# Two-layer decoder trunk on one core: gate columns' product, trips, residual and first loads rescheduled; spread of maxima 128 rows deep; gate statistics turned by two products

## The chip, the cores and the metric

The kernel runs on 1 core of one Trainium2 chip. The metric is the time of one execution in microseconds; the median of 3 runs of the kernel before is 1042.13 us (1041.74 to 1042.76).

## The reference

A sequence of 256 tokens, 2048 features wide, passes two layers. All is float32.

```python
hn = rmsnorm(h, norm)
# layer 0: u = hn @ e_w_in (six column groups: q, f, i, za, xb, zb of 1024)
ya = head_rmsnorm(hgrn2(q, f, i), a_norm) * silu(za)   # gated linear recurrence, 8 heads
yb = rg_lru(causal_conv(xb)) * silu(zb)                # elementwise recurrence
h = h + concat(ya, yb) @ e_w_out
# layer 1: u = hn @ o_w_in (qk 2048, v 2048, og 2048, z 2048, ig 8, fg 8)
li = ig + c_b_i;  lf = log_sigmoid(fg + c_b_f)
yc = mlstm(silu(conv(qk)), v, li, lf)                  # matrix memory, running-max stabiliser
yc = head_rmsnorm(yc, c_norm) * sigmoid(og) * silu(z)
h = h + yc @ o_w_out
# after each layer's mixer
pl = rmsnorm(p[i] @ ple_w[i], ple_norm[i])
h = h + sigmoid(h @ ple_gate_w[i]) * pl
# at the end: rmsnorm(h, final_norm)
```

The 16 gate columns `ig`, `fg` of the second layer give per head a log input gate and a log forget gate. From them come, per head and token, the running maximum `Mx`, the exponents `av` and the floor `enm` of the denominator.

## The kernel before, in words

**The large products.** Every weight matrix is cut into quarters of 128 partitions by 2048 values, each loaded by `load_weights` as two transfers of 512 KB into `raw` (5 buffers) on the queue of SyncE (SP). Each float32 weight is split into `whi` (a cast on ScalarE, L132) and `wlo` (raw minus whi, on VectorE, L133); the activations are split the same way. `quarter_tok` then issues three matmuls for each pair of 128 features and half of the tokens: hi x hi (L193), hi x lo (L194), lo x hi (L195), each 128 rows deep and 512 columns wide. A block of 512 output columns (`project_tok`) is four quarters, 96 matmuls. `whi` and `wlo` have 4 buffers each, so two quarters.

**Who sets the order.** The program is written for a scheduler that puts each engine's instructions into one fixed stream. Side work is written as generators in named lanes; `pump()`, called once in each quarter, advances every lane by one step, and places what the step emits behind the last instruction of TensorE, ScalarE, VectorE and the last trip (`last["pe"]`, `last["act"]`, `last["dve"]`, `last["hop"]`). `tc.issue_after(x)` puts an instruction behind `x` in the order.

**Trips.** Between token-major and feature-major layout a block goes out to DRAM and back (`across`, L452 the store, L455 four loads), issued by GpSimd (POOL). A trip's user continues after `lag` steps of its lane. `gated_mix` (L804) multiplies the trip of `zb` with the recurrence's result; `feature_major` (L483) scales and splits the other half of the first mixer's output.

**The start.** `embed` multiplies the first 256-wide input with two weight blocks `pw` of 2048 columns. The first block is loaded in pieces (four of 256 columns, two of 512), some on ScalarE's queue (`s`), the rest on SP's (`sy`); the first half of the second block in two pieces of 512, the last in one of 1024. Then come the blocks of `ew`.

**The end of layer 0.** `hq` is the residual, four blocks of 512 KB loaded by POOL at L865. `out_proj` adds the product `eo` to it (L374, on VectorE). Behind the first `eo` block the space of pool `m0` is closed and used again by pool `e0`: the rows of gains (`row`, L322, loaded by POOL, used at L329), the gate columns `gr` (L882, loaded by SP) and `wg` (L885, VectorE: `gr` times the norm's gains). `wg` is used first by `gate_sums` (L896), in the block after `eo`.

**The gate statistics.** `gate_stats` computes `li`, `lf`, `Mx`, `av`, `enm` as 8 rows of 256 and turns `av` and `enm` to tokens x heads by four small float32 products with the identity (L1001, 8 rows deep; a float32 product is two passes in the trace). `split_rows` puts `Mx` into rows 0 to 7 and its rounding rest into rows 32 to 39 of the tile `s`, rows 8 to 31 are zero. For each pair of heads `spread` (L233) copies one head's row to all 128 partitions by a product of 40 rows with `identr`, twice for each of the four calls of `mix`; L1052 are the products with the values that stand ahead of the next pair's spread.

Of the kernel before, what the change touches and what calls it, by code (L numbers as in the profile page):

```python
# [11 lines left out]
F32 = mybir.dt.float32  # L12
# [4 lines left out]
ALU = mybir.AluOpType  # L17
# [26 lines left out]
def trunk(ctx: ExitStack, tc: tile.TileContext, a, out):  # L44
# [72 lines left out]
        return pc(name, 0, PRM[name][1])  # L117


    def load_weights(src, pieces=(1, 1), queues=8 * (sy,)):  # L120
        parts = []
        for hf in range(2):
            raw = wp.tile([P, 1024], F32, name="raw", tag="raw", bufs=5)
            hi = wp.tile([P, 1024], F32R, name="whi", tag="whi")
            lo = wp.tile([P, 1024], F32R, name="wlo", tag="wlo")
            n = 1024 // pieces[hf]
            for c in range(0, 1024, n):
                r, h, l = (x[:, c:c + n] for x in (raw, hi, lo))
                queues[hf * 4 + c // n].dma_start(out=r, in_=src[:, hf * 1024 + c:hf * 1024 + c + n])
                with ExitStack() as order:  # L130
                    order.enter_context(tc.high_priority(offset=400))
                    last["act"] = s.copy(h, r).ins  # L132
                    last["dve"] = v.tensor_tensor(out=l, in0=r, in1=h.bitcast(F32), op=ALU.subtract).ins  # L133
            parts.append((hi, lo))
        return parts
# [86 lines left out]

    def split_rows(x):

        both = tp.tile([P, T], F32R, name="s8", tag="dg", bufs=1)[0:40]
        v.memset(both.bitcast(F32), 0.0)
        v.tensor_copy(both[0:8], x)
        v.tensor_tensor(out=both[32:40], in0=x, in1=both[0:8].bitcast(F32), op=ALU.subtract)
        return both

    def spread(o, both, h):

        te.matmul(o, identr[:, h:h + 1].to_broadcast([40, P]), both, start=True, stop=True)  # L233

    def free_copy(rt, name):
        ps = to_free(rt)
# [35 lines left out]
    def embed(w, pact, tile_of, first=None):  # L272

        pls = []
        for b in range(2):
            head = first and b == 0
            parts = load_weights(w[b], *((((4, 2), (s, s) + 6 * (sy,)) if head else ((2, 1),)) if first else ()))
            if first and b:
                first()
            for c, (hi, lo) in enumerate(parts):  # L280
                terms = [(hf, k, x, y) for hf in range(2) for k in range(2) for x, y in ((0, 0), (0, 1), (1, 0))]
                if head:
                    terms.sort(key=(lambda t: (t[3], t[3] and t[0], t[1])) if c == 0 else
                               (lambda t: (t[1], t[3] if t[1] == 0 else t[0], t[3])))
                pool, name = (px, "mx") if head and c == 0 else (pm, "mm")
                ps = [pool.tile([P, 512], F32, name=name, tag=name) for _ in range(2)]
                halves = []
                for n, (hf, k, x, y) in enumerate(terms):
                    mine = [m for m, t in enumerate(terms) if t[0] == hf]
                    with ExitStack() as behind:  # L290
                        if first and "pe" in last:
                            behind.enter_context(tc.issue_after(last["pe"]))
                        last["pe"] = te.matmul(ps[hf], tokens(pact[x], k, hf), (hi, lo)[y][:, k * 512:(k + 1) * 512],  # L293
                                               start=(n == mine[0]), stop=(n == mine[-1])).ins
                    if n < mine[-1]:
                        continue
                    pl = tile_of()
                    with ExitStack() as order:
                        if first:
                            order.enter_context(tc.high_priority(offset=600))  # L300
                        if hf and (b or not first):
                            v.tensor_copy(pl, ps[hf])
                        else:
                            s.copy(pl, ps[hf])
                    halves.append(pl)
                pls.append(halves)
        return pls
# [87 lines left out]
    def small(n, name, rows=P):  # L395
# [7 lines left out]
    m0 = m0_scope.enter_context(tc.tile_pool(name="m0", bufs=2))  # L403
    pls = embed(a["pw"], load_p(0), lambda: p0.tile([P, 512], F32, name="pl", tag="pl"),
                lambda: sy.dma_start(out=prm, in_=a["prm"]))
    identr = cp.tile([40, 8], F32R, name="identr")
    acth = []
    xt = [hp.tile([P, 1024], F32, name="xt", tag="h") for _ in range(4)]
    xss = cp.tile([P, 2, 2], F32, name="xss")
# [50 lines left out]
    def landed(u, name, lag):  # L460

        w = room("w")
        w5 = w.rearrange("p (j c h t) -> p h c j t", j=4, c=4, h=2)
        for hf in range(2):
            v.transpose(w5[:, hf], u[hf].rearrange("p (c j q) -> p c j q", c=4, j=4))  # L465
        r = room("r")
        yield from across(w, r, name, lag)
        return r
# [72 lines left out]
    if True:  # L541
# [254 lines left out]

        def gated_mix(j, u):

            r = yield from landed((u[:, 0], u[:, 1]), f"dzb{j}", 6 - j)
            while ("h", j) not in res:  # L800
                yield
            for b in range(2):
                x = tp.tile([P, 512], F32, name="xr", tag="hn", bufs=3)
                v.tensor_tensor(out=in_order(x, 0, 2), in0=as_read(r, 2 * b, 2),  # L804
                                in1=in_order(res["h", j], 2 * b, 2), op=ALU.mult)
                y[4 + 2 * j + b] = split_act(x, "y")
# [12 lines left out]
        def combine():  # L819
            for g in [g for g in held if ("o", g) in res]:  # L820
                u = held.pop(g)
                for hf in range(2):
                    v.tensor_tensor(out=u[:, hf], in0=u[:, hf], in1=res["o", g][:, hf], op=ALU.mult)
                start(f"fm{g}", feature_major(u, "an", 4 * g, y, 5))

        for g in range(2):
            start(f"f{g}", f_use(g, scaled_tok(2 * g, None if g else load_x)))
# [31 lines left out]
            step(f"fm{2 + g}")  # L859
        drain("rg", "pl")  # L860
    hq = []
    for i in range(4):
        t = hp.tile([P, 2, 512], F32, name="hq", tag="h")
        with tc.issue_after(last["hop"]):
            gp.dma_start(out=t, in_=a["x"].rearrange("(h p) f -> p h f", h=2)[:, :, i * 512:(i + 1) * 512])  # L865
        hq.append(t)

    def mixed():
        for c, ps in enumerate(chunks(a["eo"], 4, y, ready(y, "fm"))):
            if c == 0:  # L870
                m0_scope.close()
                pe0.append(l0.enter_context(tc.tile_pool(name="e0", bufs=1)))
                start("pg", ple_gain(pls, row(pe0[0], "row", 2, 0)))
            yield ps
# [7 lines left out]
    sy.dma_start(out=gr, in_=a["ogf"])  # L882
    wt = e0.tile([P, KT, 32], F32, name="wg")
    gp.memset(wt, 0.0)
    v.tensor_tensor(out=wt[:, :, 0:16], in0=gr, in1=pall("on").unsqueeze(2).to_broadcast([P, KT, 16]), op=ALU.mult)  # L885
    gps = px.tile([P, 512], F32, name="mx", tag="mx")

    held5 = []
# [32 lines left out]
    with tc.tile_pool(name="m1", bufs=2) as m1:  # L921
# [45 lines left out]
            return m1.tile([8, T], F32, name=name, bufs=1)  # L967

        li, xf, ab, Bc, Mx = (t8(n) for n in ("li", "xf", "ab", "Bc", "Mx"))
        lf, av, enm = xf, li, Bc  # L970
        aT = m1.tile([P, 32], F32, name="aT", bufs=1)
        pM = []

        def gate_stats():
            yield
            ps = px.tile([P, 512], F32, name="mx", tag="mx")
            te.matmul(ps[0:40, 0:T], gsum, gm, start=True, stop=True)
            cbi = prm[0:8, PRM["cbi"][0]:PRM["cbi"][0] + 1]
            cbf = prm[0:8, PRM["cbf"][0]:PRM["cbf"][0] + 1]
            for x, c, b in ((li, 0, cbi), (xf, 32, cbf)):  # L980
                v.tensor_tensor(out=x, in0=ps[c:c + 8, 0:T], in1=norm["rs"][c:c + 8], op=ALU.mult)
                v.tensor_scalar(x, x, b, None, op0=ALU.add)
            s.activation(ab, xf, AF.Abs)
            s.activation(ab, ab, AF.Exp, scale=-1.0)
            v.tensor_scalar(ab, ab, 1.0, None, op0=ALU.add)
            s.activation(ab, ab, AF.Ln)
            v.scalar_tensor_tensor(lf, xf, 0.0, ab, op0=ALU.min, op1=ALU.subtract)
            v.tensor_tensor_scan(Bc, ones[0:8, :], lf, 0.0, op0=ALU.mult, op1=ALU.add)
            v.tensor_tensor(out=av, in0=li, in1=Bc, op=ALU.subtract)
            v.tensor_tensor_scan(Mx, ones[0:8, :], av, 0.0, op0=ALU.mult, op1=ALU.max)  # L990
            v.tensor_tensor(out=enm, in0=Bc, in1=Mx, op=ALU.add)
            s.activation(enm, enm, AF.Exp, scale=-1.0)
            pM.append(split_rows(Mx))
            yield
            yield
            yield
            px_ = px.tile([P, 512], F32, name="mx", tag="mx")
            for c, x in ((0, av), (16, enm)):
                for hf in range(2):
                    o = c + hf * 8  # L1000
                    te.matmul(px_[:, o:o + 8], x[:, hf * P:(hf + 1) * P], ident[0:8, 0:8], start=True, stop=True)  # L1001
            v.tensor_copy(aT, px_[:, 0:32])

        start("mix", gate_stats())

# [333 lines left out]
```

## Time and profile before

| | |
|---|---|
| median of 3 runs | 1042.13 us (1041.74 to 1042.76) |
| the profiled execution's own time | 1042.44 us |
| its span in the trace | 1040.7 us |
| TensorE busy | 1030.2 us, 99% |
| weight loads busy | 854.7 us, 82% |
| VectorE busy | 730.4 us, 70% |
| ScalarE busy | 601.7 us, 58% |
| GpSimd busy | 90.1 us, 9% |
| HBM read, written | 216.02 MB, 17.83 MB |

Times in a trace count from the span's start. A matmul's start is recorded, its end is modelled, and matmuls overlap, so that the distance from one start to the next tells the rate, not the duration. "PEld" is TensorE loading weights. A bracket behind a row is the engine's idle time ahead of it and what ended that.

### The profile page before, as it was taken

The numbers are of one execution on the slowest core, as the hardware profiler recorded it, in microseconds if no ns is written. First come the engines' busy times: TensorE is split into PE (matmuls) and PEld (weight loads), VectorE is DVE, ScalarE is ACT, GpSimd is POOL, SyncE is SP. The second block draws the span as 40 slices with busy tenths as digits, with TensorE's granted clock in tenths as the row PEclk, the third lists the DMA queues.
The fourth block names the chain that finished last, engine by engine and source line by source line (L and its number), as shares of the span: only waits on it lengthen the run. The fifth ranks groups of instructions, "written<-read, shape, count | busy, mean of one in ns | idle before, by whom it ended". The sixth has DMA issues, their size and how long they took to land.

```text
span 1040.7 us, 14521 instructions
## 1 busy us (share of the span) xinstructions
PE 1030.2 (99%) x5278; PEld 854.7 (82%) x5278; DVE 730.4 (70%) x1101; ACT 601.7 (58%) x887; POOL 90.1 (9%) x171
## 2 busy tenths in 40 slices
PE   9999999999999999999999999999999999999996
PEld 7888888888888888888788788888888888888886
DVE  7858878969685775777569976555457777666675
ACT  7675555587974444565557765644445557344553
POOL 0111101001121211111021000000001110111000
PEclk9999999999999999999999999999999999999999
DMA  9977646567779877687587654455557778788552
GB/s 343 342 246 228 222 160 210 179 202 232 234 247 313 288 248 242 212 276 239 179 268 253 201 173 153 162 183 186 198 195 230 247 257 284 240 251 247 195 182 82
DMA packets 67752, 234.80 MB, mean 226 GB/s; under 512 B 8800, under 2 KB 10080, under 8 KB 67680
## 3 DMA queue, kind: packets, MB, share of 16 engines
q1 hardware_dynamic: 55728, 196.64, 56.9%
q0 software_dynamic: 11520, 36.71, 11.7%
q8 instruction: 41, 0.67, 0.3%
q10 hardware_dynamic: 432, 0.52, 0.1%
q14 instruction: 31, 0.25, 0.1%
HBM read 216.02 MB, written 17.83 MB: 225 GB/s over the span
## 4 chain that ended last, share of the span: by engine, by line
PE 91%; issue 4%; DMA 2%; ACT 1%; POOL 1%; DVE 0%; ACTq 0%; DVEq 0%; POOLq 0%; SPq 0%
PE mm L193 25%; PE mm L194 25%; PE mm L195 25%; PE mx L195 3%; PE mx L193 3%; PE mx L194 3%; PE mm L293 2%; DMA gr<-in_ogf_dram 1%; PE nu L1052 1%; DMA r<-dzb 1%; PE mm L1180 1%; PE mm L1179 1%; PE mm L1178 1%; DMA dzb<-w 1%; POOL r L455 1%
## 5 line engine op out<-in xcount | busy, mean ns | idle before, releaser
L133 DVE TENSOR_TENSOR wlo<-raw,whi 128x1024 fp32r<-128x1024 f32 (+2 forms) x365 | 437.7, 1207 | 228.7 <-ACT whi L132 215.9
L132 ACT CAST whi<-raw 128x1024 fp32r<-128x1024 f32 (+2 forms) x365 | 378.9, 1041 | 328.5 <-PE mm L195 260.0
L193 PE MATMUL mm<-whi,ahl 128*128 128x512 f32 x1216 | 475.6, 391 | 0.0
L194 PE MATMUL mm<-wlo,ahl 128*128 128x512 f32 x1216 | 473.8, 390 | 0.4 <-DVE wlo L133 0.4
L195 PE MATMUL mm<-whi,ahl 128*128 128x512 f32 x1216 | 473.3, 389 | 0.0
L193 PEld LDWEIGHTS mm<-whi,ahl 128*128 128x128 f32 x1216 | 228.3, 188 | 49.3 <-issue 1.2
L194 PEld LDWEIGHTS mm<-wlo,ahl 128*128 128x128 f32 x1216 | 228.3, 188 | 48.2 <-DVE wlo L133 2.0
L195 PEld LDWEIGHTS mm<-whi,ahl 128*128 128x128 f32 x1216 | 228.2, 188 | 47.8
L193 PE MATMUL mx<-whi,ahl 128*128 128x512 f32 x160 | 62.4, 390 | 0.0
L195 PE MATMUL mx<-whi,ahl 128*128 128x512 f32 x160 | 62.3, 389 | 0.0
L194 PE MATMUL mx<-wlo,ahl 128*128 128x512 f32 x160 | 62.3, 389 | 0.0
L195 PEld LDWEIGHTS mx<-whi,ahl 128*128 128x128 f32 x160 | 30.0, 188 | 6.3
L194 PEld LDWEIGHTS mx<-wlo,ahl 128*128 128x128 f32 x160 | 30.0, 188 | 6.3
L193 PEld LDWEIGHTS mx<-whi,ahl 128*128 128x128 f32 x160 | 30.0, 188 | 6.2
L452 POOL DMA_DIRECT2D ducn<-w x4 | 2.2, 560 | 221.4 <-DVE w L465 221.4
L944 DVE SCALAR_TENSOR_TENSOR qk<-xr,prm,qk 128x255 f32<-128x255 f32 (+2 forms) x48 | 20.3, 471 | 0.1
L147 DVE TENSOR_TENSOR ahl<-xr,ahl 128x512 fp32r<-128x512 f32 x24 | 16.3, 685 | 4.1 <-ACT ahl L146 4.0
L1179 PE MATMUL mm<-wlo,ahl 128*128 128x256 f32 x64 | 18.1, 283 | 0.0
L1180 PE MATMUL mm<-whi,ahl 128*128 128x256 f32 x64 | 18.1, 283 | 0.0
L1178 PE MATMUL mm<-whi,ahl 128*128 128x256 f32 x64 | 18.1, 283 | 0.0
L293 PE MATMUL mm<-whi,ahl 128*128 128x512 f32 x56 | 17.6, 391 | 0.0
L146 ACT CAST ahl<-xr 128x512 fp32r<-128x512 f32 x24 | 14.7, 612 | 4.0 <-DVE xr L804 3.9
(316 smaller groups left out, 811.6 us busy)
## 6 DMA issues: line engine op xcount, KB each, us to landing
raw<-in_ew_dram SPq DMA_DIRECT2D x64, 512.0 KB, 5.3
raw<-in_g_dram SPq DMA_DIRECT2D x56, 512.0 KB, 4.7
raw<-in_eo_dram SPq DMA_DIRECT2D x32, 512.0 KB, 6.0
raw<-in_oqk_dram SPq DMA_DIRECT2D x32, 512.0 KB, 4.8
raw<-in_ov_dram SPq DMA_DIRECT2D x32, 512.0 KB, 4.0
raw<-in_oog_dram SPq DMA_DIRECT2D x32, 512.0 KB, 3.9
raw<-in_oz_dram SPq DMA_DIRECT2D x32, 512.0 KB, 4.1
raw<-in_oo_dram SPq DMA_DIRECT2D x32, 512.0 KB, 4.9
```

Source lines behind the costliest of these rows:

```text
L132: last["act"] = s.copy(h, r).ins
L133: last["dve"] = v.tensor_tensor(out=l, in0=r, in1=h.bitcast(F32), op=ALU.subtract).ins
L146: (v.tensor_copy if name == "p0" else s.copy)(hi, src)
L147: v.tensor_tensor(out=lo, in0=src, in1=hi.bitcast(F32), op=ALU.subtract)
L193: te.matmul(ps[hf], xh, wh, start=(k == 0), stop=False)
L194: te.matmul(ps[hf], xh, wl, start=False, stop=False)
L195: last["pe"] = te.matmul(ps[hf], xl, wh, start=False, stop=(k == KT - 1)).ins
L293: last["pe"] = te.matmul(ps[hf], tokens(pact[x], k, hf), (hi, lo)[y][:, k * 512:(k + 1) * 512], start=(n == mine[0]), stop=(n == mine[-1]) ...
L944: v.scalar_tensor_tensor(dst[:, sh:T], pi[:, 0:T - sh], pc("ccw", k * 16 + n), dst[:, sh:T], op0=ALU.mult, op1=ALU.add)
L1178: te.matmul(ps[hf], xh, wh, start=(k == 0), stop=False)
L1179: te.matmul(ps[hf], xh, wl, start=False, stop=False)
L1180: last["pe"] = te.matmul(ps[hf], xl, wh, start=False, stop=(k == KT - 1)).ins
```

## The change

Six edits, none of which changes what is computed:

1. **First loads.** The pieces of the first `pw` block go to ScalarE's queue and SP's in turn; the second block is loaded as two pieces of 1024.
2. **Spread.** The tile `s` and `identr` have 128 rows, rows 40 to 127 zero; the product takes all 128.
3. **Turned statistics.** `av` and `enm` are rows 0 to 7 and 32 to 39 of one tile `ae` of 40 rows that is zeroed first. Two products turn it, and two copies take the columns out.
4. **Trips.** The lag of the second `gated_mix` goes from 5 to 6, that of `feature_major` with the gains `an` from 5 to 6.
5. **Residual.** Only two blocks of `hq` are loaded at the old place, the third and fourth after the second and third block of `eo`, each behind the trip last issued then.
6. **Gate columns' product.** `wg` is placed behind the last split of the program so far.

```diff
-    def load_weights(src, pieces=(1, 1), queues=8 * (sy,)):
+    def load_weights(src, pieces=(1, 1), queues=(sy,)):
...
-                queues[hf * 4 + c // n].dma_start(out=r, in_=src[:, hf * 1024 + c:hf * 1024 + c + n])
+                queues[c // n % len(queues)].dma_start(out=r, in_=src[:, hf * 1024 + c:hf * 1024 + c + n])
...
-        both = tp.tile([P, T], F32R, name="s8", tag="dg", bufs=1)[0:40]
+        both = tp.tile([P, T], F32R, name="s8", tag="dg", bufs=1)
...
-        te.matmul(o, identr[:, h:h + 1].to_broadcast([40, P]), both, start=True, stop=True)
+        te.matmul(o, identr[:, h:h + 1].to_broadcast([P, P]), both, start=True, stop=True)
...
-            parts = load_weights(w[b], *((((4, 2), (s, s) + 6 * (sy,)) if head else ((2, 1),)) if first else ()))
+            parts = load_weights(w[b], *(((4, 2), (s, sy)) if head else ()))
...
-    identr = cp.tile([40, 8], F32R, name="identr")
+    identr = cp.tile([P, 8], F32R, name="identr")
...
-            r = yield from landed((u[:, 0], u[:, 1]), f"dzb{j}", 6 - j)
+            r = yield from landed((u[:, 0], u[:, 1]), f"dzb{j}", 6)
...
-                start(f"fm{g}", feature_major(u, "an", 4 * g, y, 5))
+                start(f"fm{g}", feature_major(u, "an", 4 * g, y, 6))
...
-    for i in range(4):
+
+    def load_hq(i, behind):
         t = hp.tile([P, 2, 512], F32, name="hq", tag="h")
-        with tc.issue_after(last["hop"]):
+        with tc.issue_after(behind):
             gp.dma_start(out=t, in_=a["x"].rearrange("(h p) f -> p h f", h=2)[:, :, i * 512:(i + 1) * 512])
         hq.append(t)
 
+    for i in range(2):
+        load_hq(i, last["hop"])
+
     def mixed():
         for c, ps in enumerate(chunks(a["eo"], 4, y, ready(y, "fm"))):
+            if c in (1, 2):
+                load_hq(c + 1, last["hop"])
...
-    v.tensor_tensor(out=wt[:, :, 0:16], in0=gr, in1=pall("on").unsqueeze(2).to_broadcast([P, KT, 16]), op=ALU.mult)
+    with tc.issue_after(last["dve"]):
+        v.tensor_tensor(out=wt[:, :, 0:16], in0=gr, in1=pall("on").unsqueeze(2).to_broadcast([P, KT, 16]), op=ALU.mult)
...
-        lf, av, enm = xf, li, Bc
+        lf = xf
+        ae = m1.tile([40, T], F32, name="ae", bufs=1)
+        av, enm = ae[0:8], ae[32:40]
...
+            v.memset(ae, 0.0)
...
-            for c, x in ((0, av), (16, enm)):
-                for hf in range(2):
-                    o = c + hf * 8
-                    te.matmul(px_[:, o:o + 8], x[:, hf * P:(hf + 1) * P], ident[0:8, 0:8], start=True, stop=True)
-            v.tensor_copy(aT, px_[:, 0:32])
+            for hf in range(2):
+                te.matmul(px_[:, hf * 40:hf * 40 + 40], ae[:, hf * P:(hf + 1) * P], ident[0:40, 0:40],
+                          start=True, stop=True)
+            for c, o in ((0, 0), (16, 32)):
+                v.tensor_copy(aT[:, c:c + 16].rearrange("p (h n) -> p h n", h=2),
+                              px_[:, 0:80].rearrange("p (h n) -> p h n", h=2)[:, :, o:o + 8])
```

In the stream of TensorE, at the gate statistics and the first spread (`mx` is a PSUM tile, `cst` holds the identity, `li` and `Bc` hold `av` and `enm`), stood before:

```order
L195 MATMUL mm<-whi,ahl 128x512
L1001 MATMUL mx<-cst,li 128x8 x2
L1001 MATMUL mx<-cst,Bc 128x8 x2
L233 MATMUL mx<-s_5379,identr 128x256 x2
L193 MATMUL mm<-whi,ahl 128x512
```

There stands now:

```order
L195 MATMUL mm<-whi,ahl 128x512
L1009 MATMUL mx<-cst,ae 128x40 x2
L233 MATMUL mx<-s_5378,identr 128x256 x2
L193 MATMUL mm<-whi,ahl 128x512
L194 MATMUL mm<-wlo,ahl 128x512
```

Two products are gone, and nothing else moved there.

In the stream of VectorE, in the first block of `eo` (`xr` is `gated_mix`, `ahl` its split, `wlo` the weights' low parts, `wg` the gate columns' product, `hq` the residual's sum), stood before:

```order
L133 TENSOR_TENSOR wlo<-raw,whi 128x1024 x4
L804 TENSOR_TENSOR xr<-r,tt 128x512 x2
L147 TENSOR_TENSOR ahl<-xr,ahl 128x2x256 x2
L133 TENSOR_TENSOR wlo<-raw,whi 128x1024 x2
L885 TENSOR_TENSOR wg<-gr,prm 128x16x16
L133 TENSOR_TENSOR wlo<-raw,whi 128x1024 x4
L329 TENSOR_TENSOR pl<-pl,row 128x512
L374 TENSOR_TENSOR hq<-mm,hq 128x512
```

There stands now:

```order
L133 TENSOR_TENSOR wlo<-raw,whi 128x1024 x6
L804 TENSOR_TENSOR xr<-r,tt 128x512 x2
L147 TENSOR_TENSOR ahl<-xr,ahl 128x2x256 x2
L133 TENSOR_TENSOR wlo<-raw,whi 128x1024 x4
L329 TENSOR_TENSOR pl<-pl,row 128x512
L374 TENSOR_TENSOR hq<-mm,hq 128x512
```

`gated_mix` comes two splits later, and `wg` has left this place; it stands in the third block of `eo`, two splits ahead of the fourth block's sum. On SP the load of `gr` likewise moves two loads back.

In the stream of ScalarE, at the start (`pl` is the embedding's result, copied out of PSUM), stood before:

```order
L129 DMA raw<-in_pw_dram 128x256 x2
L132 ACT_TABLE_LOAD
L132 CAST whi<-raw 128x256 x4
L132 CAST whi<-raw 128x512 x3
L304 COPY pl<-mx 128x512 x2
L132 CAST whi<-raw 128x512
L132 CAST whi<-raw 128x1024
L304 COPY pl<-mm 128x512 x2
L254 ACTIVATE ahl<-xq,prm 128x256 x3
L304 COPY pl<-mm 128x512
```

There stands now:

```order
L129 DMA raw<-in_pw_dram 128x256 x2
L129 DMA raw<-in_pw_dram 128x512
L132 ACT_TABLE_LOAD
L132 CAST whi<-raw 128x256 x4
L132 CAST whi<-raw 128x512 x2
L132 CAST whi<-raw 128x1024
L304 COPY pl<-mx 128x512 x2
L132 CAST whi<-raw 128x1024
L304 COPY pl<-mm 128x512
L254 ACTIVATE ahl<-xq,prm 128x256
L304 COPY pl<-mm 128x512
```

The second block's first cast is one of 1024 columns ahead of the copies, where two of 512 stood on both sides of them, and an activation's split stands between two copies.

## The prediction

> **What bounds the kernel now.** I read the page first: busy time by engine, granted clock, and the chain that ended last.
>
> ```profile
> PE 1030.2 (99%) x5278; PEld 854.7 (82%) x5278; DVE 730.4 (70%) x1101; ACT 601.7 (58%) x887; POOL 90.1 (9%) x171
> PEclk9999999999999999999999999999999999999999
> PE 91%; issue 4%; DMA 2%; ACT 1%; POOL 1%; DVE 0%; ACTq 0%; DVEq 0%; POOLq 0%; SPq 0%
> ```
>
> TensorE (PE) is busy all along at full clock, and 91% of the chain is its own. An edit on another engine can pay only where that engine makes TensorE wait. Next, TensorE's waits (microseconds in total, times, longest), all there are:
>
> ```profile
> PE st L96 <- POOL ones L91: 1.1, 1, 1.1
> PE mm L194 <- DVE wlo L133: 0.4, 1, 0.4
> ```
>
> The first is a warm-up at the start that the change leaves alone. So the gain can't come from named waits alone; what else there is lies in the spacing of starts, which "busy" hides. TensorE's timeline gives the yardstick and the second wait's place:
>
> ```profile
> 333.23 0.39 PE L194 MATMUL mx<-wlo,ahl 128*128 128x512 f32 x1
> 333.46 0.39 PE L195 MATMUL mx<-whi,ahl 128*128 128x512 f32 x1
> 333.69 0.39 PE L193 MATMUL mm<-whi,ahl 128*128 128x512 f32 x1
> 334.44 0.50 PE L194 MATMUL mm<-wlo,ahl 128*128 128x512 f32 x1 [0.36 <-DVE wlo L133]
> 334.77 0.39 PE L195 MATMUL mm<-whi,ahl 128*128 128x512 f32 x1
> ```
>
> A product of 512 columns starts 0.23 us after the one before. From L193 to L195 two steps should take 0.46; they took 334.77 - 333.69 = 1.08. The loss is 0.62, more than the 0.36 in the bracket, since the refilling counts too. All terms below are such differences of starts.
>
> **The gate columns' product: 0.62.** VectorE's timeline, and SP's around it:
>
> ```profile
> 332.82 0.43 DVE L885 TENSOR_TENSOR wg<-gr,prm 128x256 f32<-128x256 f32 x1 [7.46 <-DMA gr<-in_ogf_dram]
> 321.20 0.33 SPq L882 DMA_DIRECT2D gr<-in_ogf_dram  x1
> ```
>
> `wg` held VectorE for 7.46 us, and the splits `wlo` queued behind it. TensorE lost only 0.62 of this: VectorE was 7.46 - 0.62 = 6.8 us ahead. Moved into the third block of `eo`, `wg` finds `gr` landed long before, and its 0.43 us lie under that lead. `gr`'s own load goes two loads back on SP, to a place where nothing reads it for tens of microseconds. I take the whole 0.62. What is late next: the trip product L804, which moves two splits back; two splits are two times 1.23 us (row below) on VectorE plus the casts they follow, some 5 us, and it then has the cover of the 7.46 us that are gone. At no gain the term is 0.
>
> **The spread: 1.14.** TensorE, then its weight loads, at the second pair of heads; `40*128` is rows by columns of the weights:
>
> ```profile
> 612.34 0.28 PE L1052 MATMUL nu<-vt,sl 128*128 128x258 f32 x1
> 612.46 0.28 PE L1052 MATMUL nu<-vl,sh 128*128 128x256 f32 x1
> 612.66 0.50 PE L233 MATMUL mx<-s,identr 40*128 40x256 f32 x2
> 613.09 0.50 PE L193 MATMUL mm<-whi,ahl 128*128 128x512 f32 x1
> 613.43 0.39 PE L194 MATMUL mm<-wlo,ahl 128*128 128x512 f32 x1
> 612.66 0.29 PEld L233 LDWEIGHTS mx<-s,identr 40*128 40x128 f32 x2
> 613.09 0.19 PEld L193 LDWEIGHTS mm<-whi,ahl 128*128 128x128 f32 x1
> 613.20 0.19 PEld L194 LDWEIGHTS mm<-wlo,ahl 128*128 128x128 f32 x1
> ```
>
> Between products of 128 rows, 256 columns take 0.12 (612.34 to 612.46). Into the 40 rows it is 0.20, and out of them the weights of L193 load at 613.09, with the product and not ahead of it, whereas L194's load at 613.20 precedes its product at 613.43. From 612.46 to 613.43 there are 0.97; steadily it would be three steps of 0.12 and one of 0.23, so 0.59. The loss is 0.38, at three pairs (the first stands below): 1.14. The product is as wide as before, only deeper, and the zeros are written once by the memset that was there. I read the loss as that of a change of depth, which 128 rows avoid. Bounds: 0, if the loss has another cause, and 1.14.
>
> The Trainium skill weighs in on both sides. TensorEngine Tiling (Array Packing), Key Properties, says that a change of tiling mode drains TensorE; the late loads agree, though no row names a mode. TensorE: Matmul & The Clock Gate, Step-by-step, says that the row count doesn't matter for the weight load and that the throughput is the number of columns alone; by that the term would be 0. The extra 0.38 beside products of nearly equal width speaks against it, but doesn't prove depth.
>
> **The turned statistics and the first pair: 0.65.**
>
> ```profile
> 591.21 0.61 PE L1001 MATMUL mx<-cst,li 8*128 8x8 f32 x4
> 591.67 0.59 PE L1001 MATMUL mx<-cst,Bc 8*128 8x8 f32 x4
> 592.19 0.50 PE L233 MATMUL mx<-s,identr 40*128 40x256 f32 x2
> 592.62 0.50 PE L193 MATMUL mm<-whi,ahl 128*128 128x512 f32 x1
> 592.96 0.39 PE L194 MATMUL mm<-wlo,ahl 128*128 128x512 f32 x1
> ```
>
> Four passes take 591.67 - 591.21 = 0.46. Four of eight go: 0.46. The four that stay are 40 columns wide in place of 8; even 256 take 0.12, so they cost no more. Behind them the spread takes 592.96 - 592.19 = 0.77 where two steps of 0.12 and one of 0.23 make 0.46 (with rounding), a drain of 0.31. It goes on leaving the spread, but the turn stays shallow, so a change of depth stays on entering it; I charge one step, 0.12, and keep 0.19. Together 0.65; if depth is nothing, 0.46. The memset of `ae` and the second small copy are on VectorE under the lead of 6.8 us.
>
> **The trips: 0.20.** TensorE and ScalarE (ACT) in the first layer:
>
> ```profile
> 283.59 0.39 PE L195 MATMUL mm<-whi,ahl 128*128 128x512 f32 x1
> 283.92 0.50 PE L193 MATMUL mm<-whi,ahl 128*128 128x512 f32 x1
> 284.25 0.40 PE L194 MATMUL mm<-wlo,ahl 128*128 128x512 f32 x1
> 281.70 0.50 ACT L483 ACTIVATE xr<-r,prm 128x256 f32<-128x256 f32 x1
> 283.19 0.68 ACT L853 ACTIVATE u<-mm,rcr 128x512 f32<-128x512 f32 x1
> ```
>
> 284.25 - 283.59 = 0.66, against 0.46: 0.20 lost, while L853 was reading out the PSUM tile. L483, 0.50 long, stood ahead of it on ScalarE. With the longer lag L483 comes behind it, and the release is 0.50 earlier, more than the 0.20. I take 0.20, with 0 below if another read ends last there. POOL's next trip load then waits a little longer, which no product does within its block.
>
> **The residual: 0.** The two moved loads now stand behind trips on POOL. The first goes about where the second store of `dfe` stood:
>
> ```profile
> 352.03 0.57 POOL L452 DMA_DIRECT2D dfe<-w  x1
> DMA to landing us min/median/max: 9.0/11.9/14.9
> 364.58 0.68 DVE L374 TENSOR_TENSOR hq<-mm,hq 128x512 f32<-128x512 f32 x1
> ```
>
> (The middle row is for the four loads of `hq`.) From 352.03 to its use at 364.58 are 12.55 us; the worst landing, 14.9, would stop VectorE for 2.4, under its lead of 6.8. The store behind it goes some 0.7 later. The last block has 20 us more before its use. At SP's loads two blocks of 512 KB fewer compete at the start of `eo`, where TensorE waits for none. So 0.
>
> **The first loads: 0.1.**
>
> ```profile
> 5.34 2.12 PE L293 MATMUL mx<-whi,ahl 128*128 128x512 f32 x8
> 12.05 0.82 PE L293 MATMUL mm<-whi,ahl 128*128 128x512 f32 x2
> 12.72 0.39 PE L293 MATMUL mm<-wlo,ahl 128*128 128x512 f32 x1
> 8.36 0.62 ACT L132 CAST whi<-raw 128x512 fp32r<-128x512 f32 x1 [0.55 <-DMA raw<-in_pw_dram]
> 9.84 0.63 ACT L132 CAST whi<-raw 128x512 fp32r<-128x512 f32 x1
> 10.79 1.05 ACT L132 CAST whi<-raw 128x1024 fp32r<-128x1024 f32 x1 [0.33 <-DMA raw<-in_pw_dram]
> 11.88 1.23 DVE L133 TENSOR_TENSOR wlo<-raw,whi 128x1024 fp32r<-128x1024 f32 x1 [0.68 <-ACT whi L132]
> ```
>
> The 24 products of the first block run from 5.34 to some 10.9 (24 times 0.23); then the second block's first split is needed. As one piece of 1024 its cast takes 1.05 and its low part 1.23. If it lands when the old first piece did, 8.36, it is ready at 10.6, in time; if only when the second did, 9.84, at 12.1, and TensorE loses up to 1.1. For a gain there are the early pieces in two queues, an estimated 0.2, and the 12.05 to 12.72 hole (0.67 for two starts plus 0.21), together up to 0.5. I take 0.1, nearer to no change, since both ends are about as near.
>
> **Sum.** 0.62 + 1.14 + 0.65 + 0.20 + 0.1 = 2.71. The profiled execution took 1042.44 us, 1.7 more than its span and 0.3 more than the median of the runs, 1042.13. I expect 1039.7 for such an execution and 1039.4 for the median.
>
> **Rivals.** *Depth is not the cause.* The products of 40 rows drain because they differ in another way (the weights there are one column repeated). Then 1.14 and 0.19 stay: 2.71 - 1.33 = 1.38, and 1040.7. For it: no row shows a spread of 128 rows. Against: the extra steps stand on both sides of the shallow rows and nowhere beside them. *The start gets worse.* The second block's piece lands late, 1.1 lost in place of 0.1 gained: 2.71 - 1.2 = 1.5, and 1040.6. For it: the cast row shows ScalarE already waiting 0.55 for that load. Against: it is now issued one slot earlier. *The third `hq` block lands late (slower).* Its place is L374 at 364.58; VectorE's lead ends at 12.55 + 6.8 = 19.4 us after issue, and from there each microsecond is TensorE's. At twice the longest landing, 29.8, it costs 10.4; less 2.7 that is +7.7, or 1049.8. Slower by 0.2% needs a landing over 24.2. Against: one load alone, where four at once took 14.9 at most.
>
> **How the numbers follow.** About 0.2%, 2.1 us, is what a measurement of this kernel can tell from no change: faster lies below 1040.0, slower above 1044.2. Forecast 0.66, depth 0.16, start 0.11, late residual 0.07. The forecast lies 0.6 below the bound, so a few hundredths of it fall within 0.2%, as do nearly all of the second and third: faster 0.62, same 0.31, slower 0.07. The range: below, the start's better end (0.4 more than taken) and the spread of the runs (the lowest, 1041.74, is 0.4 under their median), with 0.2 for rounded starts, 1038.4; above, the depth rival with the trips at 0 (1041.0) and 0.4 for the spread of the runs, 1041.4. The slow rival is left out.
>
> **What would show it.** In the changed profile: L194 follows L193 by 0.23 where `wg` no longer stands; the weight load of L233 ahead of its product and about 0.59 from the last L1052 to L194 at three pairs; two passes for each of two turned products; no 0.20 behind L853; TensorE's second embedding block without a hole over 0.2. It is wrong if the spread keeps 0.97, if a new wait on `hq`, `zb`'s trip or the second `pw` block is named, or if the lead of VectorE proves shorter than 6.8.

## The result, and the profile after

| | before | changed |
|---|---|---|
| median | 1042.13 us (1041.45 to 1043.4, 19 runs) | 1040.19 us (1039.83 to 1041.26, 19 runs) |
| profiled span | 1040.7 us | 1038.7 us |
| TensorE busy | 1030.2 us | 1028.5 us |

The ratio is 0.998, with a 95% interval of 0.9974 to 0.9986: 1.94 us faster, 0.19%, with the interval on both sides of the 0.2% that the prediction named. It had said 1039.4, in 1038.4 to 1041.4. The median lies 0.2 above the 1040.0 below which the prediction, with a chance of 0.62, put a faster kernel, so in the part to which it gave 0.31, and nearer to the times of its two rivals, 1040.7 and 1040.6, than to its own. The number alone doesn't speak for the mechanism; the profiles and the experiments have to.

The page of the changed kernel, busy times and the chain that ended last:

```profile
PE 1028.5 (99%) x5274; PEld 854.3 (82%) x5274; DVE 730.6 (70%) x1102; ACT 600.6 (58%) x886; POOL 90.4 (9%) x171
PE 94%; DVE 2%; ACT 2%; issue 1%; DMA 0%; SPq 0%; ACTq 0%; DVEq 0%
```

TensorE still bounds the kernel. Laying the starts of its products side by side, one by one, the distance between the two profiled executions changes at these places only:

| place | predicted | changed profile against before's |
|---|---|---|
| first loads, to 20 us | -0.1 | +0.50 |
| trips, 268 to 284 us | -0.20 | -0.07 |
| `wg`, 334 us | -0.62 | -0.66 |
| statistics and first spread, 591 us | -0.65 | -0.61 |
| three later spreads | -1.14 | -1.22 |
| sum | -2.71 | -2.06 |

The table looks like two small misses, at the start and at the trips. The experiments show that it isn't so: the first row and that of `wg` belong to the one profiled execution of before.

The second pair's spread in the changed kernel, TensorE and then its weight loads:

```profile
611.62 0.28 PE L1063 MATMUL nu<-vl,sh 128*128 128x256 f32 x1
611.74 0.40 PE L233 MATMUL mx<-s,identr 128*128 128x256 f32 x2
611.98 0.40 PE L193 MATMUL mm<-whi,ahl 128*128 128x512 f32 x1
612.21 0.40 PE L194 MATMUL mm<-wlo,ahl 128*128 128x512 f32 x1
611.63 0.31 PEld L233 LDWEIGHTS mx<-s,identr 128*128 128x128 f32 x2
611.86 0.19 PEld L193 LDWEIGHTS mm<-whi,ahl 128*128 128x128 f32 x1
```

From the last product with values to L194 there are 612.21 - 611.62 = 0.59, as forecast, against 0.97. Both weight loads now run ahead of their products (611.63 before 611.74, 611.86 before 611.98); with 40 rows they ran with them.

The statistics and the first pair:

```profile
590.66 0.39 PE L195 MATMUL mm<-whi,ahl 128*128 128x512 f32 x1
590.98 0.64 PE L1009 MATMUL mx<-cst,ae 40*128 40x40 f32 x4
591.54 0.50 PE L233 MATMUL mx<-s,identr 128*128 128x256 f32 x2
591.88 0.40 PE L193 MATMUL mm<-whi,ahl 128*128 128x512 f32 x1
592.11 0.40 PE L194 MATMUL mm<-wlo,ahl 128*128 128x512 f32 x1
```

The four passes of 40 columns and the step out of them take 591.54 - 590.98 = 0.56. From the first spread to L194 there are 0.57, against 0.77.

### The profile page after: what moved, and what is told of

Read it like the earlier page. It is cut to its first block, busy times and chain, and to the rows that moved or that the text cites. A ratio compares the mean times of both kernels' runs of the same rounds, so it can differ in the third digit from the quotient of the medians.

```text
span 1038.7 us, 14510 instructions
## 1 busy us (share of the span) xinstructions
PE 1028.5 (99%) x5274; PEld 854.3 (82%) x5274; DVE 730.6 (70%) x1102; ACT 600.6 (58%) x886; POOL 90.4 (9%) x171
## 4 chain that ended last, share of the span: by engine, by line
PE 94%; DVE 2%; ACT 2%; issue 1%; DMA 0%; SPq 0%; ACTq 0%; DVEq 0%
PE mm L193 25%; PE mm L194 25%; PE mm L195 25%; PE mx L195 3%; PE mx L193 3%; PE mx L194 3%; PE mm L293 2%; DVE wlo L133 1%; PE nu L1063 1%; PE mm L1191 1%; PE mm L1190 1%; PE mm L1189 1%; ACT whi L132 1%; PE mx L601 0%; DMA raw<-in_pw_dram 0%
## 5 line engine op out<-in xcount | busy, mean ns | idle before, releaser
L133 DVE TENSOR_TENSOR wlo<-raw,whi 128x1024 fp32r<-128x1024 f32 (+1 forms) x364 | 437.5, 1210 | 234.7 <-ACT whi L132 222.4
L132 ACT CAST whi<-raw 128x1024 fp32r<-128x1024 f32 (+1 forms) x364 | 378.2, 1043 | 325.6 <-PE mm L195 259.5
L193 PE MATMUL mm<-whi,ahl 128*128 128x512 f32 x1216 | 475.3, 391 | 0.0
L194 PE MATMUL mm<-wlo,ahl 128*128 128x512 f32 x1216 | 473.3, 389 | 0.1
L195 PE MATMUL mm<-whi,ahl 128*128 128x512 f32 x1216 | 472.9, 389 | 0.0
L193 PEld LDWEIGHTS mm<-whi,ahl 128*128 128x128 f32 x1216 | 228.3, 188 | 48.7 <-issue 1.2
L195 PEld LDWEIGHTS mm<-whi,ahl 128*128 128x128 f32 x1216 | 228.2, 188 | 47.7
L194 PEld LDWEIGHTS mm<-wlo,ahl 128*128 128x128 f32 x1216 | 228.3, 188 | 47.2 <-DVE wlo L133 0.7
L193 PE MATMUL mx<-whi,ahl 128*128 128x512 f32 x160 | 62.4, 390 | 0.0
L195 PE MATMUL mx<-whi,ahl 128*128 128x512 f32 x160 | 62.3, 389 | 0.0
L194 PE MATMUL mx<-wlo,ahl 128*128 128x512 f32 x160 | 62.3, 389 | 0.0
L194 PEld LDWEIGHTS mx<-wlo,ahl 128*128 128x128 f32 x160 | 30.0, 188 | 6.2
L195 PEld LDWEIGHTS mx<-whi,ahl 128*128 128x128 f32 x160 | 30.0, 188 | 6.3
L193 PEld LDWEIGHTS mx<-whi,ahl 128*128 128x128 f32 x160 | 30.0, 188 | 6.2
```

The lines of the kernel that those rows point to most:

```text
L193: te.matmul(ps[hf], xh, wh, start=(k == 0), stop=False)
L194: te.matmul(ps[hf], xh, wl, start=False, stop=False)
L195: last["pe"] = te.matmul(ps[hf], xl, wh, start=False, stop=(k == KT - 1)).ins
```

## The experiments

**The kernel before, profiled once more** (no edit).

> The kernel before once more, for its profile. Theory (the stall of 0.62 behind the gate columns' product and the fast start belong to the one execution that was profiled): the load of the gate columns lands in 9 to 10 us and not in 11.5, the product waits about 5 us, under VectorE's lead, and no step of TensorE near 334 is over 0.25; at the start 512 columns take 0.43 for some products instead of 0.23. Rival (both belong to the kernel): a wait of about 7.5 and a step of 1.08 again.

Its time was 1042.43, its span 1040.6. VectorE's timeline, and the load of the gate columns:

```profile
331.32 0.42 DVE L885 TENSOR_TENSOR wg<-gr,prm 128x256 f32<-128x256 f32 x1 [5.30 <-DMA gr<-in_ogf_dram]
DMA to landing us min/median/max: 9.4/9.4/9.4
```

The load landed in 9.4 us and not in 11.5, the wait was 5.30, and TensorE's steps at 334 were all 0.23. So the stall of 0.62 belonged to the execution of the first profile. The span was still the same, because this execution lost 0.62 elsewhere: by 20 us it was that much behind the first, nearly all of it in one step at 16.7. The expectation on the start failed in its form: here 512 columns took 0.23 from the second product on.

**`wg` alone.** In the code cuts from here on, `...` marks what is left out; each time is set against before's, measured beside it.

```diff
-    v.tensor_tensor(out=wt[:, :, 0:16], in0=gr, ...)
+    with tc.issue_after(last["dve"]):
+        v.tensor_tensor(out=wt[:, :, 0:16], in0=gr, ...)
```

> The kernel before with the gate columns' product alone moved behind the last split. Theory: TensorE's step of 1.08 us behind the first block of the residual's product becomes 0.46, so 0.6 to 0.7 below before, 1041.5. Rival (the trip product is late in its place): under 0.3 less.

1042.46 against 1042.12 for before on the same chip, ratio 1.0002 (0.9993 to 1.0011): nothing that shows, though by the interval alone 0.6 us could still be there. The profiles decide. This one has the step at 334 gone, 0.66 less than in the first profile of before; but so have all kernels below in which `wg` stands at its old place. VectorE's row in three of them, the spread alone, the two lags alone, and the residual alone:

```profile
330.65 0.43 DVE L885 TENSOR_TENSOR wg<-gr,prm 128x256 f32<-128x256 f32 x1 [4.86 <-DMA gr<-in_ogf_dram]
330.75 0.42 DVE L885 TENSOR_TENSOR wg<-gr,prm 128x256 f32<-128x256 f32 x1
326.87 0.42 DVE L891 TENSOR_TENSOR wg<-gr,prm 128x256 f32<-128x256 f32 x1 [1.23 <-DMA gr<-in_ogf_dram]
```

With before's loads around it `wg` waits 4.86 to 5.47 us in five profiles, under the lead of 6.8 that the prediction worked out, and TensorE loses nothing; at 7.46 it lost 0.62. The lead fits both, and the wait beyond it was the exception: one of six profiles with `wg`, its load and those around it as in before. The last two rows show more: the lags alone and the residual's edit alone each shorten that wait anyway, to 0 and to 1.23. Three edits removed the same stall, which is ordinarily not there.

**The spread alone**: 128 rows in place of 40 in `s`, `identr` and the product.

```diff
-        both = tp.tile([P, T], F32R, name="s8", tag="dg", bufs=1)[0:40]
+        both = tp.tile([P, T], F32R, name="s8", tag="dg", bufs=1)
...
-        te.matmul(o, identr[:, h:h + 1].to_broadcast([40, P]), both, ...)
+        te.matmul(o, identr[:, h:h + 1].to_broadcast([P, P]), both, ...)
...
-    identr = cp.tile([40, 8], F32R, name="identr")
+    identr = cp.tile([P, 8], F32R, name="identr")
```

> The kernel before with the spread of 128 rows alone. Theory (a change of depth drains TensorE): from the last product with values to the second product behind the spread 0.57 to 0.60 us at three pairs where there was 0.97, so 1.2 less there, and 0.2 less at the first pair, where the statistics of 8 rows still stand ahead: 1.4 below before, 1040.7. Rival (the weights are one column repeated, which stays so, or depth does not matter): no change, 1042.1.

1040.65 against 1042.33, ratio 0.9985 (0.9976 to 0.9994). In its profile the first pair gained 0.20 and the others 0.39, 0.42 and 0.42: 1.43 as expected. The weights are still one column repeated, so that rival falls.

**The spread 64 rows deep**: the same edit with 64 in place of 128.

```diff
-        both = tp.tile([P, T], F32R, name="s8", tag="dg", bufs=1)[0:40]
+        both = tp.tile([P, T], F32R, name="s8", tag="dg", bufs=1)[0:64]
...
```

> The kernel before with the spread 64 rows deep in place of 40, zeros below. Theory (any depth other than the 128 rows of its neighbours drains): 0.95 to 0.97 us from the last product with values to the second behind the spread, as with 40 rows, and the time of before, 1042.1. Rival (the cost falls with the rows that are missing): about 0.84, so 0.4 less over the three pairs, 1041.7.

1042.29 against 1042.12, ratio 0.9999 (0.9991 to 1.0008). TensorE at the second pair:

```profile
612.01 0.28 PE L1052 MATMUL nu<-vl,sh 128*128 128x256 f32 x1
612.22 0.50 PE L233 MATMUL mx<-s,identr 64*128 64x256 f32 x2
612.64 0.50 PE L193 MATMUL mm<-whi,ahl 128*128 128x512 f32 x1
612.99 0.39 PE L194 MATMUL mm<-wlo,ahl 128*128 128x512 f32 x1
```

0.98, as with 40 rows. The price is that of being different from the neighbours, not of the missing rows.

**The turned statistics alone.**

```diff
-            for c, x in ((0, av), (16, enm)):
-                for hf in range(2):
-                    te.matmul(px_[:, o:o + 8], x[:, hf * P:(hf + 1) * P], ident[0:8, 0:8], ...)
...
+            for hf in range(2):
+                te.matmul(px_[:, hf * 40:hf * 40 + 40], ae[:, hf * P:(hf + 1) * P], ident[0:40, 0:40], ...)
...
```

> The kernel before with the statistics turned by two products alone, the spread still 40 rows deep. Theory: four passes of 0.115 go, 0.46, and the turn and the first spread now have the same 40 rows, so that one drain of about 0.1 between them goes too: 0.46 to 0.6 below before, 1041.6. Rival (a product of 40 columns costs more than one of 8): under 0.3.

1041.67 against 1042.33, ratio 0.9995 (0.9986 to 1.0003); in its profile 0.55 less at 591, all of it there. The time alone wouldn't settle it, the profile does. TensorE there:

```profile
590.71 0.63 PE L1002 MATMUL mx<-cst,ae 40*128 40x40 f32 x4
591.17 0.48 PE L233 MATMUL mx<-s,identr 40*128 40x256 f32 x2
```

Here the turn and the spread behind it both have 40 rows, and 591.17 - 590.71 = 0.46 is four passes of 0.115 with nothing between them. In the changed kernel, where the spread has 128 rows, it was 0.56. So the 40 rows cost nothing by themselves; it is the change of depth that does.

**The spread and the turned statistics, nothing else.**

> The kernel before with the spread of 128 rows and the two turned products, and nothing else. Theory (the other four edits are worth nothing in an ordinary execution): 1.8 below before, 1040.3, the time of the changed kernel within 0.2. Rival (the gate columns' edit is worth its 0.62 in the median too): 1040.9 or more.

1040.39 against 1042.47, ratio 0.9981 (0.9972 to 0.999): 2.08 less. It has the changed kernel's time within 0.2, and so the other four edits together are worth nothing that shows; the intervals leave room for some tenths.

**The two lags alone.**

```diff
-            r = yield from landed((u[:, 0], u[:, 1]), f"dzb{j}", 6 - j)
+            r = yield from landed((u[:, 0], u[:, 1]), f"dzb{j}", 6)
...
-                start(f"fm{g}", feature_major(u, "an", 4 * g, y, 5))
+                start(f"fm{g}", feature_major(u, "an", 4 * g, y, 6))
```

> The kernel before with the two lags alone. Theory (the scheduler also puts one product that was ahead of the waiting one behind it, so that TensorE comes to the wait one step earlier): the 0.20 us at 283.6 to 284.3 stay, and the time is that of before within 0.1, 1042.1. Rival (the prediction's): 0.20 less.

1042.38 against 1042.12, ratio 1.0003 (0.9994 to 1.0012). At 284 its profile stands as before did, within 0.02. What the lags do gain, 0.07, stands at 268.5, in this profile and in every other with the new lags. There the weights of one product came late in before, as the view of the weight loads says:

```profile
268.17 0.19 PEld L194 LDWEIGHTS mm<-wlo,ahl 128*128 128x128 f32 x1 [0.19 <-DVE wlo L133]
```

With the new lags they wait for nothing. Why nothing is gained at 284 is seen in the changed kernel, TensorE and then ScalarE:

```profile
283.80 0.39 PE L194 MATMUL mm<-wlo,ahl 128*128 128x512 f32 x1
284.12 0.50 PE L193 MATMUL mm<-whi,ahl 128*128 128x512 f32 x1
284.46 0.40 PE L194 MATMUL mm<-wlo,ahl 128*128 128x512 f32 x1
283.38 0.69 ACT L853 ACTIVATE u<-mm,rcr 128x512 f32<-128x512 f32 x1
```

ScalarE does release the PSUM tile earlier, by 0.24 against TensorE's products (L853 at 283.38 after 283.19, where TensorE by then runs 0.50 - 0.07 = 0.43 later). But between L194 and the waiting L193 stood an L195 before; the scheduler has moved it behind four more groups, and TensorE comes to the wait a step of 0.23 sooner. The two cancel: 284.46 - 283.80 is 0.66 for two steps, as before.

**The residual alone**: the third and fourth block loaded behind the trips of the second and third block of `eo`.

> The kernel before with the third and fourth blocks of the residual alone loaded later. Theory: no step of TensorE changes, 1042.1. Rival: the gate columns' load, which follows on another queue, lands earlier since two blocks of 512 KB fewer compete, and the step of 1.08 us gets shorter, by up to 0.6.

1042.24 against 1042.12, ratio 1.0001 (0.9992 to 1.0009). The load of `gr` does land earlier, in 5.3 us, as the rival said; the time doesn't show it, as above. In the changed kernel all four blocks land sooner than before, with no wait at L374:

```profile
DMA to landing us min/median/max: 7.2/8.3/8.9
```

**The first loads: the changed kernel with the old ones, with both 512s on SP, and once more.**

> The changed kernel with the first loads as they were before; all else is changed. Theory (the fourth piece of 256 columns lands late, at 6.47 us and not at 5.20, because the first piece of 512 now leaves at the same time on the other queue): the fifth product starts at about 6.4 again and not at 6.95, and the time falls by the 0.5 us that the start lost, to about 1039.6, 2.5 below before. Rival (the slow start is a matter of the run, not of the loads): no difference to the changed kernel, 1040.2.

> The changed kernel with the four pieces of 256 columns still in turn on the two queues, but both pieces of 512 on SP behind them. Theory (the piece of 512 beside the fourth piece is what makes it late): the fourth piece lands at about 5.0, the first product stays at about 5.0 and the fifth starts by 6.2; the time is 0.5 to 0.8 below the changed kernel, 1039.4 to 1039.7. Rival (two queues in turn are slower for all pieces): the fourth piece still lands after 6, and the time stays 1040.2.

> The changed kernel once more, for its profile. Theory (the fourth piece of 256 columns shares the engines with the first piece of 512): it lands over 1 us later than the third again, at about 6.4, and the fifth product starts at 6.9. Rival (a matter of the run): it lands at about 5.2.

The edits to the changed kernel, first the old loads, then the split (in both, the list of queues is again read as before's):

```diff
-            parts = load_weights(w[b], *(((4, 2), (s, sy)) if head else ()))
+            parts = load_weights(w[b], *((((4, 2), (s, s) + 6 * (sy,)) if head else ((2, 1),)) if first else ()))
...
```

```diff
+            parts = load_weights(w[b], *(((4, 2), (s, sy, s, sy) + 4 * (sy,)) if head else ()))
...
```

The times are 1040.26, 1040.22 (ratios to before 0.9978, 0.997 to 0.9987, and 0.9979, 0.997 to 0.9988) and 1040.36: no difference to the changed kernel's 1040.19, against the theory of the first two. Its mechanism is there all the same. ScalarE's casts in the changed kernel and, last, with both 512s on SP:

```profile
4.14 1.08 ACT L132 CAST whi<-raw 128x256 fp32r<-128x256 f32 x3 [0.72 <-DMA raw<-in_pw_dram]
6.49 0.93 ACT L132 CAST whi<-raw 128x256 fp32r<-128x256 f32 x2 [1.26 <-DMA raw<-in_pw_dram]
4.21 1.34 ACT L132 CAST whi<-raw 128x256 fp32r<-128x256 f32 x4 [1.27 <-DMA raw<-in_pw_dram]
```

In the changed kernel the fourth piece comes 1.26 us after ScalarE is free, at 6.49, and at 6.43 in its second profile; with the 512s behind it all four are cast in a row, and the fifth product, the first that needs the third and fourth piece, starts at 6.55 in place of 6.95. Most of it is given back by 13.5 us: of the 0.52 that the split is ahead of the changed kernel at 11 us 0.17 are left, of the old loads' 0.60 only 0.09. TensorE and its weight loads: the changed kernel, the split, the old loads:

```profile
11.93 0.19 PEld L293 LDWEIGHTS mm<-wlo,ahl 128*128 128x128 f32 x1 [0.35 <-DVE wlo L133]
11.75 0.51 PE L293 MATMUL mm<-wlo,ahl 128*128 128x512 f32 x1 [0.27 <-DVE wlo L133]
13.00 0.50 PE L293 MATMUL mm<-whi,ahl 128*128 128x512 f32 x1 [0.47 <-ACT pl L304]
```

The second block's low part, or ScalarE's copy out of PSUM, is the next to be late, and a better head only lengthens that wait. Against before's first profile, ten profiles with the old loads (it among them) stand 0 to 1.1 us behind at 20 us, 0.43 in the mean; three with the new stand 0.36 to 0.54 behind, 0.47 in the mean. Edit 1 is worth nothing that these can tell.

**Two more products filled up**: the changed kernel with the turn 128 rows deep, and the gathering product with 128 columns of weights (`gw`, zeros but for `gsum`).

```diff
-        ae = m1.tile([40, T], F32, name="ae", bufs=1)
+        ae = m1.tile([P, T], F32, name="ae", bufs=1)
+        gw = m1.tile([P, P], F32, name="gw", bufs=1)
...
+            v.memset(gw, 0.0)
+            v.tensor_copy(gw[:, 0:40], gsum)
...
-            te.matmul(ps[0:40, 0:T], gsum, gm, start=True, stop=True)
+            te.matmul(ps[:, 0:T], gw, gm, start=True, stop=True)
...
-                te.matmul(..., ae[:, hf * P:(hf + 1) * P], ident[0:40, 0:40], ...)
+                te.matmul(..., ae[:, hf * P:(hf + 1) * P], ident[:, 0:40], ...)
```

> The changed kernel with two more products filled up with zeros: the turned statistics 128 rows deep, and the product that gathers the gate columns' sums 128 columns of weights wide in place of 40. Theory (every change of the rows or columns in use drains TensorE): the step into the first spread, 0.21 us, becomes 0.12, the steps around the gathering product lose 0.3 to 0.4; 0.4 to 0.6 below the changed kernel, 1039.7. Rival (only depth counts, not the columns of the weights): 0.1 to 0.2 below, 1040.0.

1039.53 (1039.22 to 1040.12), ratio to before 0.997 (0.9959 to 0.9982), 0.7 below the changed kernel's median and the lowest of all. The two intervals overlap; the profile has the difference. TensorE at the gathering product, the changed kernel and then this one, and the turn in this one:

```profile
573.55 0.39 PE L195 MATMUL mm<-whi,ahl 128*128 128x512 f32 x1
573.87 0.63 PE L987 MATMUL mx<-gm,cst 128*40 128x256 f32 x2
574.42 0.50 PE L193 MATMUL mm<-whi,ahl 128*128 128x512 f32 x1
574.76 0.39 PE L194 MATMUL mm<-wlo,ahl 128*128 128x512 f32 x1
573.59 0.39 PE L195 MATMUL mm<-whi,ahl 128*128 128x512 f32 x1
573.82 0.59 PE L990 MATMUL mx<-gm,gw 128*128 128x256 f32 x2
574.06 0.59 PE L193 MATMUL mm<-whi,ahl 128*128 128x512 f32 x1
574.48 0.40 PE L194 MATMUL mm<-wlo,ahl 128*128 128x512 f32 x1
590.62 0.53 PE L1012 MATMUL mx<-cst,ae 128*128 128x40 f32 x4
590.98 0.48 PE L233 MATMUL mx<-s,identr 128*128 128x256 f32 x2
```

From L195 to L194 there are 0.89 in place of 1.21, and the turn takes 590.98 - 590.62 = 0.36 in place of 0.56. So the columns of the weights count as the rows do: the profile has 0.31 less at the gathering product, and as much at the turn, which gained more than expected, since its entry got shorter too. Not all of the loss is gone: behind the gathering product L193 to L194 still take 574.48 - 574.06 = 0.42, where such a step is 0.23. Why, isn't shown.

## Why the prediction was right, and which of its steps were not

- **Spread, 1.14**: measured 1.22 in the changed kernel and 1.23 alone. The mechanism, time lost at a change of depth, is shown by the 128 rows, by the 64 that cost what 40 do, by the turn and the spread of 40 rows each, between which nothing is lost, and by the columns of the gathering product. The rule of the Trainium skill in TensorEngine Tiling (Array Packing), Key Properties, that a change of mode drains TensorE, fits all four, though no row names a mode. The Trainium skill's rule in TensorE: Matmul & The Clock Gate, Step-by-step, that rows don't matter, holds for the load's own duration (two loads 0.29 at 40 rows, 0.31 at 128), but not for what stands around it.
- **Turned statistics and first pair, 0.65**: measured 0.61. Two passes in place of four for each half and the loss that stays on entering the spread (0.56 against 0.46) came as worked out.
- **Gate columns, 0.62: the step that failed.** It took a stall from one execution as a property of the kernel. The wait and the lead were read rightly, but a wait only 0.7 over its cover, set by a DMA's landing, is a matter of the run: 11.5 us there, 8.7 to 9.5 in the six other profiles with the same loads around it. In an ordinary execution the term is 0.
- **Trips, 0.20: failed.** The order of ScalarE was looked at, that of TensorE at the same place was not, and the release came 0.24 earlier and not 0.50. At 284 it measured 0. The 0.07 at 268 was in no term: the two waits that the prediction called all there are were those of the products, and the weight loads' view names more.
- **First loads, 0.1**: 0 within what the runs tell, though not for the reason given. The early pieces in two queues were held for a gain of 0.2 that no row gave. The first product does start earlier, at 4.97 to 5.11 against 5.17 to 5.44 in the ten profiles with the old loads, but the first 512 beside them made the fourth piece late; the rival's late 1024 piece is what eats any gain ahead of it.
- **Residual, 0**: right, and the slow rival had no ground: landings got shorter.

With these sizes the sum is 1.22 + 0.61 + 0.07 = 1.90, and 1.94 was measured. The forecast of 2.7 was too large by 0.8, about what the gate columns, the trips and the first loads fell short by. That the time still lies in the range is owed to its width, since the range reached up to the depth rival's time. The two terms with a price paid on TensorE itself, the same in every execution, were right to 0.1.

## What to carry to other kernels

In a kernel that TensorE bounds, look at the spacing of starts around small products: where fewer than 128 rows or columns of weights are in use, zeros up to 128 cost no time on it here and took away 0.2 to 0.4 us at each such group of products. A term that rests on one landing time, against a cover of nearly the same length, is worth only the share of executions in which it is over (here one profile of six); look for a second profile. Look at the waits of the weight loads too, and not at those of the products alone: in before they name idle time of 0.4 ahead of L601, at five places, and of L673, at four, whose weights have 32 columns. What filling those up would give was not tried. When an edit moves one engine's order, read all engines' orders at that place.

## What the runs showed of the hardware

TensorE's rate at the start differs between executions though the granted clock reads 1.00 in all of them: the first eight products of 512 columns in before, and those of the kernel with `wg` alone, whose loads are the same:

```profile
5.34 2.12 PE L293 MATMUL mx<-whi,ahl 128*128 128x512 f32 x8
5.40 2.98 PE L293 MATMUL mx<-whi,ahl 128*128 128x512 f32 x8
```

In the latter the first step was 0.59 and the next three 0.43, until 7.3 us; in before the first was 0.34 and the others 0.23. The warm-up ahead of them shows it too: its last two steps are 0.11 in the kernel with the two lags alone, where all but the first are 0.21 in before. TensorE: Matmul & The Clock Gate of the Trainium skill, What's actually happening, has the clock released at the end of a window that runs freely, so that the point differs from run to run, by half a microsecond either way. The two rows agree that it differs, but by more: the slow steps end before 5.7 us in one and at 7.3 us in the other. Whether this is the cause isn't shown. Nor is what makes the gate columns' load land in 9 or in 11.5 us.
